# A decoder layer on one core: the chunk stage's loads three chunks ahead, its exponential sums from a store, and the modulation vectors made in the pair stage

## The chip, the cores and the metric

The kernel runs on one core of one Trainium2 chip. The metric is device microseconds of one execution; the median of three runs is 2089.88 us (2089.57 to 2091.57).

A core has a matrix engine (TensorE, PE in the profile; its weight loads are PEld), an elementwise engine (VectorE, DVE), an engine for functions of one input (ScalarE, ACT), a slower general one (GpSimd, POOL), and SyncE (SP), whose queue issues all of this kernel's loads and stores. Each engine runs its own queue in order, and engines wait for one another by semaphores.

## The reference

One layer, 1024 positions by 1024 channels, in float32. The parts that matter here:

```python
mod = silu(c) @ ada_w + ada_b                       # 6 vectors of 1024
sh1, sc1, gt1, sh2, sc2, gt2 = split(mod, 6)
h = rmsnorm(x, mix_pre_g) * (1.0 + sc1) + sh1
z, xbc, dt_raw, sc_b, sc_c, sc_h, gates = split(h @ w_in)
y_ssd = ssd_branch(z, xbc, dt_raw, ...) @ w_ssd_out # chunked scan, below
y_sc = short_conv_branch(sc_b, sc_c, sc_h, sc_conv_w) @ w_sc_out
mix = (sigmoid(gates)[0] * y_ssd + sigmoid(gates)[1] * y_sc) @ w_o
x = x + gt1 * rmsnorm(mix, mix_post_g)
h = rmsnorm(x, ffn_pre_g) * (1.0 + sc2) + sh2
x = x + gt2 * rmsnorm(ffn(h), ffn_post_g)
```

In the scan, 32 heads in 4 groups and 8 chunks of 128 positions; per chunk, with `a_cs` the running sum of `dt * a`:

```python
decay = exp(where(causal, a_cs[l] - a_cs[s], -inf))
y_diag = ((C @ B.T) * decay) @ x                     # within the chunk
state_new = state * exp(a_cs[-1]) + (B, exp(a_cs[-1] - a_cs), x)
y_off = (C * exp(a_cs)) @ state                      # from the chunks before
```

## The kernel before, in words

Matrix products run on operands split into a rounded high part and a remainder, three products in place of one. ScalarE casts the high part (L131), VectorE subtracts (L132). The stages, by the trace:

- **Start** (0 to 100 us): x is normalised, the vectors sc1 and sh1 are made, h is transposed.
- **Pair stage** (100 to 720): 34 times two column blocks of `w_in` are multiplied with h (class `Pair`, L179 to L277). A pair forms seven block products of twelve matmuls each from seven weights: the blocks 11, 21, 22 and the differences t1, t2, t3, t4. The split weights lie in a pool with seven buffers per kind (`ws`), so the last weight of the next pair, t4, takes the buffer that the last product of the pair before still reads. The kinds follow the string at L644: z (gate of the scan), g (merge gates), s (short convolution: two pairs sch with a multiply L629, the taps L621 on ScalarE and L624 on VectorE, then a pair scb), x (the scan's input).
- **Chunk stage** (720 to 1040): 32 chunks, n = 8 g + c. `ssd_front` transposes x and forms x·dt and the scores; `ssd_decay` forms the exponentials: a tile E, a broadcast of the running sums (L711), gives Cs = exp(E) on ScalarE (L737), and is then itself turned into the decay (L745, L746); `ssd_weigh` multiplies Cs by C and E by the masked scores on VectorE (L753, L754); `ssd_back` makes y and the state (L771, L781); `ssd_square`, `ssd_norm` (L681, L683, a power on GpSimd, L686) and `ssd_late` normalise y. Between them stand twelve projections, a half at a time by the table STEPS. x, B and C of two chunks come in one load, xb (L703), the gate in another, zt (L705), both with two buffers.
- **Passage and branches** (1040 to 1435): y is reloaded and split, and multiplied with `w_ssd` and `w_sc` (names bps). A generator `extra` is stepped between products; in it the vectors gt1, sc2, sh2 and later gt2 are made: eight loads of a 128x1024 block of `ada_w`, sixteen multiply-adds into two accumulators (L333, L335), then a matmul with ones (L359) or eight transposes (L343) and a sum.
- **Feed-forward** (1435 to 2088): 22 pairs of `w_up`, then `w_down`.

The order in the queues isn't the order of the code alone: a scheduler places each instruction on its engine by its own model of when its operands are there. A tile with several buffers makes an instruction wait for the last reader of the buffer that it takes.

Of the kernel before, what the change touches and what calls it, by code (L numbers as in the profile page):

```python
# [18 lines left out]
NG = 4  # L19
# [15 lines left out]
def hybrid_kernel(ctx: ExitStack, tc: tile.TileContext, x, pack, row_p, ada_w, w_in,  # L35
# [78 lines left out]
    acs_d = dram.tile([NCH, 32, P], F32, name="acs_d")  # L114

# [209 lines left out]
    def ada_steps(i, name, rows=False):  # L325
        r = None if rows else const.tile([P, 8], F32, name=name + "_c")
        acc = [qt(f"{name}_acc{h}") for h in range(2)]
        for k in range(KT):
            pc = load_raw(ada_w[k * P:(k + 1) * P, i * D:(i + 1) * D], f"{name}_p{k}")
            for h in range(2):  # L330
                src = pc[:, h * 512:h * 512 + 512]
                if k == 0:
                    V.tensor_scalar(acc[h], src, csil[:, 0:1], None, op0=ALU.mult)  # L333
                else:
                    V.scalar_tensor_tensor(acc[h], src, csil[:, k:k + 1], acc[h], op0=ALU.mult, op1=ALU.add)  # L335
            if k % 2:
# [17 lines left out]
    def ada_gate(i, n, name, dst=None, dram_dst=None):  # L354
        for acc in ada_steps(i, name, True):
            yield
        ps = double(f"{name}_ps")
        for h in range(2):
            PE.matmul(ps[:, h, :], ones, acc[h], start=True, stop=True)  # L359
        for h in range(2):  # L360
# [4 lines left out]
            V.tensor_tensor(b, ps[:, h, :], b, op=ALU.add)  # L365
            d = dst[:, sl] if dst is not None else b
            V.tensor_tensor(d, b, g, op=ALU.mult)
            if dst is None:
                SY.dma_start(dram_dst[:, sl], b)
# [156 lines left out]
    def dt_steps():  # L526
        nega = const.tile([P, 1], F32, name="nega")
        sts = []
        for th in range(2):
# [26 lines left out]
            st = l  # L556
            V.tensor_copy(st[0:32, :], cs[0:32, :])
# [138 lines left out]
    pairs = {}  # L696

    def ssd_front(g, c):
        nm = f"{g}_{c}"
        if c % 2 == 0:  # L700
            tsl = slice(c * P, c * P + 256)
            xb = ld.tile([P, 6, 256], F32, tag="xb", name=f"xb{nm}")
            SY.dma_start(xb, xbc_d[g][:, :, tsl])  # L703
            zt = ld.tile([P, 4, 256], F32, tag="zt", name=f"zt{nm}")
            SY.dma_start(zt, z_d[g][:, :, tsl])  # L705
            pairs["in"] = xb, zt
        xb, zt = pairs["in"]
# [56 lines left out]
    def ssd_back(front, decay):  # L764
        nm, g, c, xb, zt, cs, hs, E, xdt, sm, Bt = front
        Cs, cd, xw = decay
        state = pairs.get("state")
        pt = bank(f"y{nm}")
        for j in range(4):
            def ymm(o, lhs, rhs, first, last):  # L770
                return PE.matmul(pt[o * 64:o * 64 + 64, j * P:j * P + P], lhs[:, 2 * j + o, :], rhs[:, 2 * j + o, :],  # L771
                                 start=first, stop=last)
            for o in range(2):
                ins = ymm(o, xdt, E, True, c == 0)
            if c > 0:
                for o in range(2):
                    ins = ymm(o, state, Cs, False, True)
# [577 lines left out]
```

## Time and profile before

| | us |
|---|---|
| median of three runs (range) | 2089.88 (2089.57 to 2091.57) |
| profiled execution | 2089.95 |
| its span | 2088.2 |
| TensorE busy | 2006.3 (96%) |
| VectorE busy | 1499.0 (72%) |
| ScalarE busy | 998.2 (48%) |
| GpSimd busy | 158.0 (8%) |

The span runs from the first to the last instruction; the rest of an execution's time lies around it. The shares are means over stages with different limits, and each stage has to be read alone. In a timeline row stand the start in us, the duration, the engine, the line, the operation, out<-in by the program's names without buffer numbers, and in brackets how long the engine had been idle and what released it. The granted clock of TensorE, PEclk, is 1.00 at its full speed.

### The profile page before, as it was taken

Reading aid. Unit: us, or ns where it says so; the run is one execution under the profiler, and the core shown is the slowest. Engines: PE = TensorE matmul, PEld = TensorE weight load, DVE = VectorE, ACT = ScalarE, POOL = GpSimd, SP = SyncE. Lnnn points to the kernel's source line nnn. Section 1 sums busy time; section 2 is a strip of 40 time slices with the busy share of each in tenths; the row PEclk is TensorE's granted clock in tenths of the full one; section 3 lists DMA queues with packets and bytes.
Section 4 is the critical chain, followed back from the end, with each engine's and each line's share of the span. In section 5 each row is a group of like instructions: output and inputs, shape, how many; then the busy total and the mean of one; then the engine's idle time right before and its main releaser. Section 6 shows DMA issues by size and latency. Waiting matters only on the chain. (4 is left out here: it accounts for less than half of the span.)

```text
span 2088.2 us, 25325 instructions
## 1 busy us (share of the span) xinstructions
PE 2006.3 (96%) x9404; PEld 1598.0 (77%) x9404; DVE 1499.0 (72%) x2088; ACT 998.2 (48%) x1622; POOL 158.0 (8%) x183
## 2 busy tenths in 40 slices
PE   7999999999999998899989999998999999989997
PEld 3788888888888776666668878876888888868886
DVE  4977565677677688888787465368978777867876
ACT  4655344455445475656442253236545445544343
POOL 2200000000000033332100010013000000000002
PEclk9999999999999999989999999999999999999999
DMA  8223323232332455545588478343222222268372
GB/s 299 78 103 123 119 93 131 101 111 96 116 121 102 151 192 185 171 159 187 178 290 289 148 244 300 112 148 116 91 81 81 81 91 81 71 229 289 107 236 96
DMA packets 129580, 313.18 MB, mean 150 GB/s; under 512 B 11312, under 2 KB 40368, under 8 KB 129456
## 3 DMA queue, kind: packets, MB, share of 16 engines
q1 hardware_dynamic: 129456, 311.56, 42.9%
q8 instruction: 74, 1.21, 0.2%
q14 instruction: 50, 0.41, 0.1%
HBM read 243.75 MB, written 67.76 MB: 149 GB/s over the span
## 5 line engine op out<-in xcount | busy, mean ns | idle before, releaser
L1080 DVE SCALAR_TENSOR_TENSOR uv<-u_u,pk,uv 128x1023 f32<-128x1023 f32 (+1 forms) x88 | 107.2, 1278 | 7.4 <-ACT uv L1077 7.4
L131 ACT CAST u_t_hi<-u_t 128x512 fp32r<-128x512 f32 x88 | 54.7, 623 | 120.5 <-PE u_p L173 108.6
L131 ACT CAST wy_hi<-wy_raw 128x1024 fp32r<-128x1024 f32 x32 | 33.6, 1051 | 131.2 <-PE bps L896 94.3
L595 DVE SCALAR_TENSOR_TENSOR xv<-x_u,pk,xv 128x1023 f32<-128x1023 f32 (+2 forms) x72 | 87.1, 1278 | 4.9 <-ACT xv L592 4.9
L745 ACT ACTIVATE E<-E,tokS 128x128 f32<-128x128 f32 x256 | 79.4, 390 | 16.0 <-DMA E<-acs_d 15.6
L131 ACT CAST u_hi<-u_raw 128x512 fp32r<-128x512 f32 x66 | 41.0, 623 | 72.7 <-PE u_p L173 72.7
L132 DVE TENSOR_TENSOR u_t_lo<-u_t,u_t_hi 128x512 fp32r<-128x512 f32 x88 | 60.2, 687 | 21.3 <-ACT u_t_hi L131 21.1
L771 PE MATMUL y<-E,xdt 128*64 128x128 f32 x512 | 66.6, 294 | 5.1 <-issue 5.0
L132 DVE TENSOR_TENSOR wy_lo<-wy_raw,wy_hi 128x1024 fp32r<-128x1024 f32 x32 | 39.0, 1220 | 40.0 <-ACT wy_hi L131 40.0
L771 PE MATMUL y<-Cs,state 128*64 128x128 f32 x448 | 61.5, 291 | 0.0
L737 ACT ACTIVATE Cs<-E 128x1024 f32<-128x1024 f32 x28 | 29.6, 1056 | 61.2 <-DMA E<-acs_d 61.2
L131 ACT CAST x_t_hi<-x_t 128x512 fp32r<-128x512 f32 x48 | 30.0, 624 | 59.2 <-PE x_p L173 33.8
L771 PEld LDWEIGHTS y<-E,xdt 128*64 128x64 f32 x512 | 44.4, 143 | 17.7 <-issue 14.9
L1077 ACT ACTIVATE uv<-u_u,pk 128x1024 f32<-128x1024 f32 x44 | 52.5, 1239 | 2.3 <-DVE u_u L261 1.7
L1227 POOL TENSOR_TENSOR dss<-dss,dss 128x1 f32<-128x1 f32 x8 | 3.8, 476 | 623.6 <-PE dx L1155 600.2
L668 POOL MEMSET mask<- 128x128 f32 x1 | 0.2, 204 | 656.4 <-PE x_p L174 656.4
L131 ACT CAST x_hi<-x_raw 128x512 fp32r<-128x512 f32 x36 | 22.5, 624 | 52.8 <-PE x_p L173 25.0
L132 DVE TENSOR_TENSOR x_t_lo<-x_t,x_t_hi 128x512 fp32r<-128x512 f32 x48 | 32.4, 686 | 21.1 <-ACT x_t_hi L131 21.1
L771 PEld LDWEIGHTS y<-Cs,state 128*64 128x64 f32 x448 | 45.2, 145 | 2.3 <-issue 1.7
L132 DVE TENSOR_TENSOR u_lo<-u_raw,u_hi 128x512 fp32r<-128x512 f32 x66 | 44.9, 682 | 2.5 <-ACT u_hi L131 2.5
L257 DVE TENSOR_TENSOR u_u<-u_p,u_q 128x512 f32<-128x512 f32 x22 | 15.2, 691 | 43.9 <-PE u_p L174 43.9
L743 POOL TENSOR_TENSOR xw<-xdt,tokS 128x512 f32<-128x512 f32 x28 | 41.8, 1496 | 46.7 <-DVE xdt L718 46.7
(1985 smaller groups left out, 6808.6 us busy)
## 6 DMA issues: line engine op xcount, KB each, us to landing
u_raw<-in_w_up_dram SPq DMA_DIRECT2D x44, 512.0 KB, 3.5
E<-acs_d SPq DMA_DIRECT2D x32, 512.0 KB, 4.5
wy_raw<-in_w_ssd_dram SPq DMA_DIRECT2D x32, 512.0 KB, 5.0
x_raw<-in_w_in_dram SPq DMA_DIRECT2D x24, 512.0 KB, 3.5
xbc_d<-xv SPq DMA_DIRECT2D x24, 512.0 KB, 2.8
xb<-xbc_d SPq DMA_DIRECT2D x16, 768.0 KB, 5.4
f_d<-uv SPq DMA_DIRECT2D x22, 512.0 KB, 2.6
dm<-f_d SPq DMA_DIRECT2D x44, 256.0 KB, 6.0
```

Of the source, the lines that this page charges most:

```text
L131: S.copy(hi, src)
L132: V.tensor_sub(lo, src, hi.bitcast(F32))
L257: V.tensor_tensor(self.out(1, 1), self.bank(1), self.q["5"], op=ALU.add)
L595: V.scalar_tensor_tensor(v[:, s:], u[:, :T - s], w[:, k:k + 1], v[:, s:], op0=ALU.mult, op1=ALU.add)
L668: G.memset(mask, 1.0)
L737: S.activation(Cs, E, AF.Exp)
L743: G.tensor_tensor(xw, xdt, bc(tS[:, 3, hs], 64), op=ALU.mult)
L745: S.activation(E[:, h, :], E[:, h, :], AF.Relu, scale=-1.0, bias=tS[:, 0, g * 8 + h:g * 8 + h + 1])
L771: return PE.matmul(pt[o * 64:o * 64 + 64, j * P:j * P + P], lhs[:, 2 * j + o, :], rhs[:, 2 * j + o, :], start=first, stop=last)
L1077: S.activation(v, us[j], AF.Identity, scale=w[:, 2:3], bias=cv["ffn_b"][:, t:t + 1])
L1080: V.scalar_tensor_tensor(v[:, s:], us[j][:, :T - s], w[:, k:k + 1], v[:, s:], op0=ALU.mult, op1=ALU.add)
L1227: G.tensor_tensor(ss, ss, other, op=ALU.add)
```

## The change

It has three parts. In the chunk stage E is loaded three chunks ahead, in two halves of 256 KB that live in a pool with ten buffers; xb is loaded a pair of chunks earlier and has three buffers; zt one pair earlier. E's exponential and its product with the mask are done by halves. Cs is no longer computed from E: a second store in DRAM, eac_d, holds exp of the running sums, written in `dt_steps` by one ScalarE operation per half of the sequence, and Cs (two buffers as before) is a broadcast load of it, issued behind `ssd_back` for the chunk two ahead. The vectors gt1, sc2, sh2 and gt2 are made in the pair stage by the generator `mods`, stepped twice after every pair but the x pairs, the scb pairs and the first two; a half vector is eight multiply-adds into the one tile `scratch`, from four loads of 128x2x512, and a matmul with ones or four transposes. gt1 goes to DRAM (g1_d) and is reloaded before the output product. And the first three weights of the branches are loaded at the end of the chunk stage.

```diff
+    def ada_half(i, h, name):
+        for p in range(KT // 2):
+            pc = evt(f"{name}_p{p}").rearrange("p (m c) -> p m c", m=2)
+            SY.dma_start(pc, ada_w[p * 256:(p + 1) * 256, i * D + h * 512:i * D + h * 512 + 512]
+                         .rearrange("(m p) c -> p m c", p=P))
+            for m in range(2):
+                k = 2 * p + m
                 if k == 0:
+                    V.tensor_scalar(scratch, pc[:, m, :], csil[:, 0:1], None, op0=ALU.mult)
                 else:
+                    V.scalar_tensor_tensor(scratch, pc[:, m, :], csil[:, k:k + 1], scratch, op0=ALU.mult, op1=ALU.add)
+            if p < KT // 2 - 1:
+                yield
+    def ada_mod(i, r, name):
         for h in range(2):
+            yield from ada_half(i, h, f"{name}{h}")
+            ps = bank(f"{name}_ps{h}")
+            for j in range(4):
+                PE.transpose(ps[:, j * P:(j + 1) * P], scratch[:, j * P:(j + 1) * P], ident)
...
-    def ada_gate(i, n, name, dst=None, dram_dst=None):
+    def ada_gate(i, n, name, dst):
         for h in range(2):
+            yield from ada_half(i, h, f"{name}{h}")
+            ps = bank(f"{name}_ps{h}")
+            PE.matmul(ps, ones, scratch, start=True, stop=True)
...
+            kept(S.activation(e[0:32, :], cs[0:32, :], AF.Exp))
+            SY.dma_start(eac_d[th * 4:th * 4 + 4].rearrange("c h l -> h c l"),
+                         e[0:32, :].rearrange("h (c l) -> h c l", c=4))
...
+    def mods():
+        yield from ada_gate(2, 0, "gt1", g1_d)
+        yield from ada_mod(4, mod2["sc2"], "sc2")
+        plus_one(mod2["sc2"], "ffn_pre_g")
+        yield from ada_mod(3, mod2["sh2"], "sh2")
+        yield from ada_gate(5, 1, "gt2", g_d)
+    mod_it = mods()
+    for n, kind in enumerate("zzgsgsgsgsgsgsggxxzxzxxzxxzxxzxxzx"):
         fn, g, j = dict(z=zs, x=xs, g=gs, s=scs)[kind].pop(0)
         fn(g, j)
+        if n > 1 and kind != "x" and not (kind == "s" and g):
+            next(mod_it, None)
+            next(mod_it, None)
...
+            xb = ld.tile([P, 6, 256], F32, tag="xb", name=f"xb{g}_{c}", bufs=3)
...
+                t = qt(f"E{g}_{c}_{q}")
+                SY.dma_start(t, acs_d[c, h0:h0 + 4, :].rearrange("h l -> (h l)").partition_broadcast(P))
...
+            Cs = sw.tile([P, 8, P], F32, tag="Cs", name=f"Cs{g}_{c}", bufs=2)
+            SY.dma_start(Cs.rearrange("p h l -> p (h l)"),
+                         eac_d[c, g * 8:g * 8 + 8, :].rearrange("h l -> (h l)").partition_broadcast(P))
...
-            S.activation(Cs, E, AF.Exp)
...
-        S.activation(E, E, AF.Exp, scale=-1.0)
-        return Cs, cd, xw
+        for q in range(2):
...
+            S.activation(E[q], E[q], AF.Exp, scale=-1.0)
...
-        V.tensor_tensor(E, E, sm.unsqueeze(1).to_broadcast([P, 8, P]), op=ALU.mult)
+        for q in range(2):
+            V.tensor_tensor(E[q], E[q], sm.unsqueeze(1).to_broadcast([P, 4, P]), op=ALU.mult)
...
     for n in range(len(chunks)):
         this = front, decay
+        load_sums(n + 3)
+        if n % 2 == 0:
+            load_x_pair(n + 2)
+        else:
+            load_z_pair(n + 1)
...
         ssd_back(*this)
+        if n:
+            load_decay(n + 2)
...
+    pre = {(1, 0, h): load_raw(w_ssd[h * 8], f"wy1_0_{h}") for h in range(2)}
+    pre[1, 0, 2] = load_raw(w_sc[0], "ws1_0")
...
-        yield from ada_gate(2, 0, "gt1", dst=G1)
-        for nm, i in (("sc2", 4), ("sh2", 3)):
...
-        yield from ada_gate(5, 1, "gt2", dram_dst=g_d)
```

What this does to the order in the queues, at three places. The numbers behind the names count the program's tiles; lines are those of the kernel that the rows are from (each stands two lower in the changed one up to the pairs).

First, VectorE's queue around the seam from pair sch1 to pair g4 (t3_lo and t4_lo belong to g4, scb0 is the pair behind it), before:

```order
L132 TENSOR_TENSOR g4_t3_lo_1668<-g4_t3_1665,g4_t3_hi_1667 128x512
L194 TENSOR_TENSOR scb0_t2_1810<-scb0_1_raw_1794,scb0_t1_1804 128x512
L132 TENSOR_TENSOR g4_t4_lo_1674<-g4_t4_1671,g4_t4_hi_1673 128x512
L629 TENSOR_TENSOR sch1_u0_1569<-sch1_u0_1569,sch1_u1_1570 128x1024
L194 TENSOR_TENSOR scb0_t3_1820<-scb0_1_raw_1794 128x512
L624 SCALAR_TENSOR_TENSOR sch1_u1_1570<-sch1_u0_1569,pk_75,sch1_u1_1570 128x1023
L624 SCALAR_TENSOR_TENSOR sch1_u1_1570<-sch1_u0_1569,pk_75,sch1_u1_1570 128x1022
```

And in the changed kernel, where the L337 operations are the sums of the half gt1_ps1:

```order
L134 TENSOR_TENSOR g4_t3_lo_1726<-g4_t3_1723,g4_t3_hi_1725 128x512
L196 TENSOR_TENSOR scb0_t2_1876<-scb0_1_raw_1860,scb0_t1_1870 128x512
L337 SCALAR_TENSOR_TENSOR scratch_172<-gt11_p2_1669,csil_170,scratch_172 128x512
L134 TENSOR_TENSOR g4_t4_lo_1732<-g4_t4_1729,g4_t4_hi_1731 128x512
L631 TENSOR_TENSOR sch1_u0_1608<-sch1_u0_1608,sch1_u1_1609 128x1024
L337 SCALAR_TENSOR_TENSOR scratch_172<-gt11_p2_1669,csil_170,scratch_172 128x512
L196 TENSOR_TENSOR scb0_t3_1886<-scb0_1_raw_1860 128x512
L626 SCALAR_TENSOR_TENSOR sch1_u1_1609<-sch1_u0_1608,pk_75,sch1_u1_1609 128x1023
L337 SCALAR_TENSOR_TENSOR scratch_172<-gt11_p3_1673,csil_170,scratch_172 128x512
L626 SCALAR_TENSOR_TENSOR sch1_u1_1609<-sch1_u0_1608,pk_75,sch1_u1_1609 128x1022
L337 SCALAR_TENSOR_TENSOR scratch_172<-gt11_p3_1673,csil_170,scratch_172 128x512
L366 TENSOR_TENSOR gt1_b1_1679<-gt1_ps1_1677,gt1_b1_1679 128x512
```

Four sums of the half came in, three of them behind g4's t4_lo, and the last two behind a tap each. TensorE's queue at the same seam, before (the first three are the last of sch1, the others the first of g4):

```order
L172 MATMUL sch1_p1_1526<-h22_7h_542,sch1_t4_hi_1522 128x512
L173 MATMUL sch1_p1_1526<-h22_7l_543,sch1_t4_hi_1522 128x512
L174 MATMUL sch1_p1_1526<-h22_7h_542,sch1_t4_lo_1523 128x512
L172 MATMUL g4_p1_1677<-h11_0h_561,g4_11_hi_1641 128x512
L173 MATMUL g4_p1_1677<-h11_0l_562,g4_11_hi_1641 128x512
```

And changed:

```order
L174 MATMUL sch1_p1_1565<-h22_7h_544,sch1_t4_hi_1561 128x512
L175 MATMUL sch1_p1_1565<-h22_7l_545,sch1_t4_hi_1561 128x512
L176 MATMUL sch1_p1_1565<-h22_7h_544,sch1_t4_lo_1562 128x512
L361 MATMUL gt1_ps1_1677<-scratch_172,ones_82 128x512
L174 MATMUL g4_p1_1735<-h11_0h_563,g4_11_hi_1699 128x512
L175 MATMUL g4_p1_1735<-h11_0l_564,g4_11_hi_1699 128x512
```

The matmul that reads scratch stands between the pairs; the same holds for gt1_ps0 (before g2), sc2_ps0 (before sch2), sc2_ps1 (sch3), sh2_ps0 (scb2), sh2_ps1 (x0_0), gt2_ps0 (x1_0) and gt2_ps1 (x2_2).

Second, VectorE's queue at a seam behind a g pair, from g6 to sch2 (g8 follows), before:

```order
L132 TENSOR_TENSOR sch2_t3_lo_2113<-sch2_t3_2110,sch2_t3_hi_2112 128x512
L194 TENSOR_TENSOR g8_t2_2244<-g8_1_raw_2228,g8_t1_2238 128x512
L132 TENSOR_TENSOR sch2_t4_lo_2119<-sch2_t4_2116,sch2_t4_hi_2118 128x512
L194 TENSOR_TENSOR g8_t3_2254<-g8_1_raw_2228 128x512
L132 TENSOR_TENSOR g8_11_lo_2231<-g8_0_raw_2226,g8_11_hi_2230 128x512
```

And changed, with the last four sums of sc2_ps0 and their reduction (L347):

```order
L134 TENSOR_TENSOR sch2_t3_lo_2193<-sch2_t3_2190,sch2_t3_hi_2192 128x512
L196 TENSOR_TENSOR g8_t2_2332<-g8_1_raw_2316,g8_t1_2326 128x512
L337 SCALAR_TENSOR_TENSOR scratch_172<-sc20_p2_2148,csil_170,scratch_172 128x512 x2
L134 TENSOR_TENSOR sch2_t4_lo_2199<-sch2_t4_2196,sch2_t4_hi_2198 128x512
L337 SCALAR_TENSOR_TENSOR scratch_172<-sc20_p3_2152,csil_170,scratch_172 128x512
L196 TENSOR_TENSOR g8_t3_2342<-g8_1_raw_2316 128x512
L337 SCALAR_TENSOR_TENSOR scratch_172<-sc20_p3_2152,csil_170,scratch_172 128x512
L347 TENSOR_REDUCE sc2_c_902<-sc2_ps0_2156 128x4
```

Two sums stand ahead of t4_lo and two behind it. Third, SP's queue in the chunk stage (group 1), before:

```order
L711 DMA E1_2_6632<-acs_d_167 128x1024
L711 DMA E1_3_6730<-acs_d_167 128x1024
L833 DMA ysc_d4_104<-scu4_6360 128x1024
L694 DMA y_d0_96<-yo0_6_6462 512x1x256
L703 DMA xb1_4_6833<-xbc_d1_89 128x6x256
L705 DMA zt1_4_6835<-z_d1_93 128x4x256
L711 DMA E1_4_6837<-acs_d_167 128x1024
```

And changed:

```order
L720 DMA xb1_4_6987<-xbc_d1_89 128x6x256
L737 DMA E1_6_0_7092<-acs_d_167 128x512
L745 DMA Cs1_3_6981<-eac_d_168 128x1024
L737 DMA E1_6_1_7094<-acs_d_167 128x512
L875 DMA ysc_d4_104<-scu4_6594 128x1024
L711 DMA y_d0_96<-yo0_6_6703 512x1x256
L737 DMA E1_7_0_7170<-acs_d_167 128x512
L745 DMA Cs1_4_7090<-eac_d_168 128x1024
```

The load of E is two to three chunks further on, in halves, and the load of Cs, which is new, runs between them for a nearer chunk.

## Rows read from the trace of the kernel before

**Rows 1.** Three stretches: length, each engine's busy us (instructions), PEclk, DMA share, GB/s

```profile
100.00:720.00 620.00, 620.00 (x2720) 507.31 (x2721) 410.91 (x561) 298.19 (x449) 0.00 (x0) 1.00 0.31 112
720.00:1040.00 320.00, 291.11 (x1942) 217.71 (x1941) 267.43 (x503) 191.65 (x431) 90.11 (x86) 0.96 0.54 181
1075.00:1435.00 360.00, 356.14 (x1584) 289.88 (x1582) 213.08 (x265) 122.50 (x162) 26.91 (x36) 1.00 0.61 210
```

**Rows 2.** Timeline of TensorE and ScalarE, seam from pair sch to g

```profile
299.82 0.39 PE L172 MATMUL g_p<-h_0h,g_hi 128*128 128x512 f32 x1
...
299.79 0.62 ACT L131 CAST g_t_hi<-g_t 128x512 fp32r<-128x512 f32 x1 [2.10 <-PE sch_p L173]
```

**Rows 3.** Timeline of VectorE at the same seam

```profile
300.45 0.69 DVE L132 TENSOR_TENSOR g_t_lo<-g_t,g_t_hi 128x512 fp32r<-128x512 f32 x1 [1.13 <-ACT g_t_hi L131]
301.06 1.22 DVE L629 TENSOR_TENSOR sch_u<-sch_u,sch_u 128x1024 f32<-128x1024 f32 x1
...
303.50 1.28 DVE L624 SCALAR_TENSOR_TENSOR sch_u<-sch_u,pk,sch_u 128x1023 f32<-128x1023 f32 x1 [0.62 <-ACT sch_u L621]
```

**Rows 4.** Timeline of TensorE and VectorE, seam from a g pair to scb

```profile
318.99 0.39 PE L172 MATMUL scb_p<-h_0h,scb_hi 128*128 128x512 f32 x1
...
319.61 0.69 DVE L132 TENSOR_TENSOR scb_t_lo<-scb_t,scb_t_hi 128x512 fp32r<-128x512 f32 x1 [1.13 <-ACT scb_t_hi L131]
320.34 0.69 DVE L194 TENSOR_TENSOR g_t<-g_raw 128x512 f32<-128x512 f32 x1
```

**Rows 5.** Vector work: timeline of two sums; lines L359, L343 (ns min/median/max)

```profile
1063.02 1.40 DVE L335 SCALAR_TENSOR_TENSOR gt_acc<-gt_p_raw,csil,gt_acc 128x512 f32<-128x512 f32 x2
...
L359 PE MATMUL gt_ps<-gt_acc,ones x8: 590/591/592, 1079.7 to 1297.6; 128*128 128x512 f32 x8
...
L343 PE MATMUL sc_ps<-ident,sc_acc x8: 270/272/275, 1119.2 to 1120.0; 128*128 128x128 f32 x8
```

**Rows 6.** Stretches in and behind TensorE's idle times, columns as in rows 1

```profile
792.70:797.80 5.10, 0.01 (x1) 0.04 (x1) 3.67 (x7) 3.11 (x9) 0.00 (x0) 0.65 0.88 266
794.20:804.40 10.20, 6.61 (x41) 5.26 (x41) 6.12 (x14) 4.28 (x11) 1.97 (x2) 0.50 0.35 116
921.20:922.60 1.40, 0.09 (x1) 0.12 (x2) 1.40 (x4) 1.40 (x5) 0.04 (x1) 1.00 0.91 265
923.90:927.30 3.40, 3.40 (x27) 2.73 (x22) 3.38 (x6) 2.85 (x7) 0.30 (x1) 0.51 0.75 247
1041.90:1049.00 7.10, 4.51 (x18) 3.46 (x19) 7.08 (x10) 6.84 (x11) 0.00 (x0) 1.00 0.71 222
1060.50:1070.70 10.20, 4.98 (x11) 3.53 (x12) 9.12 (x14) 1.04 (x1) 0.00 (x0) 0.50 0.90 296
```

**Rows 7.** Waits from 735 to 1040: engine, line, releaser, us, times, longest

```profile
DVE ym L683 <- PE half L681: 27.2, 21, 3.7
DVE rs L686 <- POOL yr L122: 12.8, 29, 1.2
DVE Cs L753 <- ACT Cs L737: 5.5, 2, 5.1
...
PE xT L716 <- DMA xb<-xbc_d: 14.8, 12, 5.1
...
SPq L711 <- PE y L771: 84.6, 20, 9.6
```

**Rows 8.** Timeline in the chunk stage: mask product, y, Cs two chunks on

```profile
1018.13 1.22 DVE L754 TENSOR_TENSOR E<-E,sm 128x1024 f32<-128x1024 f32 x1
...
846.08 0.48 PE L771 MATMUL y<-Cs,state 128*64 128x128 f32 x3
...
858.49 1.21 DVE L753 TENSOR_TENSOR Cs<-Cs,xb 128x1024 f32<-128x1024 f32 x1
```

**Rows 9.** DMA issues of the page: count, KB each, median us to landing

```profile
E<-acs_d SPq DMA_DIRECT2D x32, 512.0 KB, 4.5
```

**Rows 10.** Timeline of TensorE at the start of the branches

```profile
1064.94 0.79 PE L895 MATMUL bps<-ys_0h,ws_hi 128*128 128x512 f32 x1 [6.58 <-ACT ws_hi L131]
1066.94 0.80 PE L897 MATMUL bps<-ys_0h,ws_lo 128*128 128x512 f32 x1 [0.78 <-DVE ws_lo L132]
```

More of the change, by code (lines that the diff above doesn't have):

```diff
@@ L114, in hybrid_kernel @@
     acs_d = dram.tile([NCH, 32, P], F32, name="acs_d")
+    eac_d = dram.tile([NCH, 32, P], F32, name="eac_d")
+    g1_d = dram.tile([P, D], F32, name="g1_d")
     def rstd_from(ms, name, ready=False):
@@ L364, in ada_gate @@
             SY.dma_start(g, row_p[2 * n + 1, sl].partition_broadcast(P))
[L365 to L369, printed above, removed]
+            V.tensor_tensor(b, ps, b, op=ALU.add)
+            V.tensor_tensor(b, b, g, op=ALU.mult)
+            SY.dma_start(dst[:, sl], b)
             yield
@@ L643, in hybrid_kernel @@
     gs = [(gate_pair, 0, 2 * n) for n in range(8)]
-    for kind in "zzgsgsgsgsgsgsggxxzxzxxzxxzxxzxxzx":
+    mod2 = {nm: const.tile([P, 8], F32, name=f"{nm}_c") for nm in ("sc2", "sh2")}
+    def mods():
[6 more added lines that the diff above has]
+    for n, kind in enumerate("zzgsgsgsgsgsgsggxxzxzxxzxxzxxzxxzx"):
         fn, g, j = dict(z=zs, x=xs, g=gs, s=scs)[kind].pop(0)
         fn(g, j)
+        if n > 1 and kind != "x" and not (kind == "s" and g):
+            next(mod_it, None)
+            next(mod_it, None)
         if steps is not None:
@@ L650, in hybrid_kernel @@
             last[1] = steps is not None
+    for _ in mod_it:
+        pass
     ph.close()
@@ L694, in ssd_late @@
             SY.dma_start(y_d[g][:, :, (c - 1) * P:(c + 1) * P], yo)
-    pairs = {}
-    def ssd_front(g, c):
-        nm = f"{g}_{c}"
[L700 to L707, printed above, removed]
+    pairs, loaded = {}, {}
@@ new lines, in hybrid_kernel, with load_x_pair, load_z_pair @@
+    chunks = [(g, c) for g in range(NG) for c in range(NCH)]
+    def load_x_pair(n):
+        if n < len(chunks):
+            g, c = chunks[n]
+            xb = ld.tile([P, 6, 256], F32, tag="xb", name=f"xb{g}_{c}", bufs=3)
+            SY.dma_start(xb, xbc_d[g][:, :, c * P:c * P + 256])
+            loaded["x", n] = loaded["x", n + 1] = xb
+    def load_z_pair(n):
+        if n < len(chunks):
+            g, c = chunks[n]
+            zt = ld.tile([P, 4, 256], F32, tag="zt", name=f"zt{g}_{c}")
+            SY.dma_start(zt, z_d[g][:, :, c * P:c * P + 256])
+            loaded["z", n] = loaded["z", n + 1] = zt
@@ L708, in ssd_front @@
+    def ssd_front(n):
+        g, c = chunks[n]
+        nm = f"{g}_{c}"
+        xb, E, Cs = loaded.pop(("x", n)), loaded.pop(("E", n)), loaded.pop(("C", n), None)
         cs = slice((c % 2) * P, (c % 2) * P + P)
         hs = slice(g * 8, g * 8 + 8)
-        E = ld.tile([P, 8, P], F32, tag="E", name=f"E{nm}")
-        SY.dma_start(E.rearrange("p h l -> p (h l)"),
-                     acs_d[c, hs, :].rearrange("h l -> (h l)").partition_broadcast(P))
         tS = tokS[:, c]
@@ L839, in hybrid_kernel @@
     proj = projections()
-    chunks = [(g, c) for g in range(NG) for c in range(NCH)]
-    front = ssd_front(0, 0)
+    load_x_pair(0)
+    for n in range(3):
+        load_sums(n)
+        load_decay(n)
+    load_z_pair(0)
+    front = ssd_front(0)
     decay = ssd_decay(front)
@@ L909, in branch_weights @@
     def branch_weights(th, i, h):
-        if i == 0 and h == 1 and not th:
-            return load_split(None, f"wy{th}_{i}_{h}", ahead_raw[0])
-        return load_split(w_ssd[h * 8 + i], f"wy{th}_{i}_{h}")
+        src = w_sc[i] if h == 2 else w_ssd[h * 8 + i]
+        return load_split(src, f"wb{th}_{i}_{h}", pre.pop((th, i, h), None))
     def branches(th, Ay, As, extra, first=()):
@@ L1000, in mod_steps @@
         SY.dma_start(ysc_d[KT - 1], tail[0])
-        yield from ada_gate(2, 0, "gt1", dst=G1)
-        for nm, i in (("sc2", 4), ("sh2", 3)):
-            for mod2[nm] in ada_steps(i, nm):
-                yield
-            if nm == "sc2":
-                plus_one(mod2[nm], "ffn_pre_g")
+        yield
     def late_steps(xn):
```

83 lines of the change are left out of this document (37 added, 46 removed).

## The prediction

> **What bounds the kernel now.** I first cut the span into the kernel's stages and read the busy time of each engine in each [rows 1]. In the pair stage (100 to 720 us) TensorE is busy for all 620.00 us; VectorE works 410.91 and ScalarE 298.19. The reader is to see that this stage has no slack on TensorE: whatever makes it wait there makes the kernel longer. In the chunk stage (720 to 1040) TensorE has 291.11 of 320 and VectorE 267.43, so neither fills it and the waits between the engines decide. In the branches (1075 to 1435) TensorE is full again, 356.14 of 360. The change works on the chunk stage, where there is idle time, and pays for it in the pair stage, where there is none.
>
> Second, I read the seam between two pairs in the timeline of three engines [rows 2, 3]. TensorE goes from the last product of pair sch to the first of pair g without a gap: g starts at 299.82. The seven weight buffers of a pair make the cast of the next pair's t4 wait on ScalarE until TensorE's last reads (2.10 us, released by the L173 matmul), and VectorE's t4_lo, which needs that cast, starts only at 300.45, that is, after TensorE has already gone on. Today nobody on TensorE is waiting for t4_lo so soon. After an s pair the multiply L629 follows it to about 302.2, and the first tap L624 waits for ScalarE's L621 and starts at 303.50. After a g pair [rows 4] it is the same up to t4_lo at 319.61, with t3 at 320.34; TensorE goes on at 318.99.
>
> Third, TensorE's idle stretches with the clock granted beside and behind them [rows 6], and last the waits of the chunk stage and of the passage to the branches [rows 7 to 10].
>
> **Modulation vectors in the pair stage: the stall.** Each of the eight halves adds eight sums into the one tile scratch, and then TensorE reads scratch: a ones-matmul for gt1 and gt2, four transposes for sc2 and sh2. In the changed order this TensorE work stands in all eight cases exactly between the last matmul of one pair and the first of the next. The last sums of the half, though, stand on VectorE behind the next pair's t4_lo: two of them after a g pair, three after a z pair, and after an s pair two (sch0) or three (sch1) mixed with the multiply and the taps. Both queues run in order, so TensorE must stand still until the last sum. Two sums took 1.40 us [rows 5], 0.70 each; the t3 difference takes 0.6 to 0.69, a tap 1.2 net.
> - sch0 to g2: multiply to 302.2; one sum and t3 fit before the tap at 303.50; tap to 304.7; sum to 305.4. TensorE was free at 299.82: 5.6 us.
> - sch1 to g4: one more tap and one more sum: 5.6 + 1.2 + 0.7 = 7.5 us.
> - four seams after g pairs (g6, g8, g10, g14): t4_lo to about 320.3, sum 321.0, t3 321.6, sum 322.3, less 318.99: 3.3 us each, 13.2.
> - two seams after z pairs (z1_2, z2_2): one more sum, 4.0 each, 8.0.
>
> Together 5.6 + 7.5 + 13.2 + 8.0 = **+34.3**. Bounds: 26, 1 us less at each seam, since the ends of TensorE's rows are modelled and its free moment with them; 45, if each seam slips by the length of one more tap, 1.3.
>
> **The same: the clock.** The granted clock has two levels in the rows, 2.4 GHz (shown as 1.00) and 1.2 GHz (0.50). Behind 5.1 us without TensorE (792.7) it was 0.50 for 10.2 us. Behind 1.3 idle of 1.4 (921.2) it was 0.51 for 3.4 us. But 2.6 idle within 1041.9 to 1049.0 left it at 1.00 [rows 6]. In a stage where TensorE is full, 10.2 us at half clock lose 5.1. So the two long stalls (5.6 and 7.5) cost 5.1 each, 10.2; the six short ones (3.3 and 4.0) lie between rows that show nothing and rows that show a whole drop, so between 0 and 5.1, and I take half, 2.55: 15.3. Together **+25.5** (bounds 10.2 and 40.8).
>
> The rule of the Trainium skill that bears on this ("TensorE: Matmul & The Clock Gate", section "Part 1: The HAM clock gate") is that the slow clock is the default and that activity lifts it. By the rule each stall of this size could put TensorE back to the slow level, by the row at 1041.9 a short one need not; the first is a rival below.
>
> **The same: the work itself.** TensorE: 8 × 0.590 + 16 × 0.272 = 9.1 us [rows 5] leave one full stage and enter another: 0. VectorE: 64 sums × 0.70 = 44.8 us come to 410.91 of 620, and fit but for the last sums counted above; in the branches, where VectorE had 213.08 of 360, their going frees nothing that TensorE waited for. The 32 loads of 512 KB move to a stage where the DMA engines are 0.31 busy [rows 1]; the extra exponential of each half of the sums goes to ScalarE, at 298 of 620. I cost these at 0; if the loads were late, the sums would be, and the stall would grow, which the bound of 45 holds.
>
> **Chunk stage.** VectorE idles 320.00 − 267.43 = 52.6 us there. The largest parts [rows 7]: 27.2 for the squares' sum on TensorE (ym, 21 times), 12.8 for the power on GpSimd (rs, 29 times), 5.5 for ScalarE's exponential Cs. TensorE's own largest wait is 14.8 us for the pair load xb, 12 times, up to 5.1 us, and ym stands behind it in TensorE's queue. With xb loaded a pair earlier the 14.8 go, and I let ym fall by as much (bounds 0, if something else is late next, and 27.2). The 28 exponentials leave ScalarE, so the 5.5 go. The power (rs) is not touched. The mask product of E is cut in two, 64 of half the width: full width lasts 1.22 [rows 8] and half width 0.69 [rows 3], each overlapping the next by 0.08 (300.45 to 301.06), so 32 × (2 × 0.61 − 1.14) = +2.6. Sum −14.8 − 5.5 + 2.6 = **−17.7** (bounds +20, see rival D, and −52.6 + 12.8 + 2.6 = −37.2).
>
> The new load of Cs could become a wait. It goes out after y of the chunk two before, and has to be there when VectorE weighs it. TensorE's y ended at 846.56 in one chunk, and the Cs of two chunks on was weighed at 858.49 [rows 8]: 11.9 us, and the loads of E, of the same size, land in 4.5 [rows 9]. Normally no wait, so 0; the longest hold of SP on y was 9.6 [rows 7], and 9.6 + 4.5 = 14.1 would be 2.2 late.
>
> **Passage to the branches.** TensorE waits 6.58 us for ws_hi and 0.78 for ws_lo [rows 10], since the raw weight is issued late; and it then runs 10.2 us at 0.50 with 4.98 busy [rows 6], 2.5 lost. With the first three weights loaded before the stage this is 9.9 at most; VectorE is full there (9.12 of 10.2) and keeps a little: **−9** (bounds 0 and −12).
>
> **The sum.** The profiled execution took 2089.95 us (span 2088.2), 0.07 over the median of three runs. 2089.95 + 34.3 + 25.5 − 17.7 − 9 = **2123 us**.
>
> **Rivals.**
> B. Every one of the eight stalls drops the clock for 10.2 us: 40.8 in place of 25.5, **2138 us**. For it: the stretch at 921.2 fell to 0.51 after 1.3 us; against it: the one at 1041.9 did not.
> C, the other side. The chunk stage loses all of VectorE's idle time but rs (−37.2) and the passage its 9, while the stalls cost their 34.3 and the clock stays: 2089.95 + 34.3 − 37.2 − 9 = **2078 us**. It decides as soon as the savings exceed the stalls with their clock. For it: the loads were what ScalarE and TensorE waited for most in this stage. Against: TensorE has 291.11 us of work in the 320 at a clock of 0.96, so that a saving of 37 would need its idle time to go altogether; and the two long stalls are longer than the 5.1 us that dropped the clock at 792.7.
> D. The load of Cs takes the place of the wait removed: with two buffers it can't be ahead. 2.2 us late in each of 28 chunks would be 62; a third of them, 20, eats the 17.7 and leaves +2.3: 2089.95 + 34.3 + 25.5 + 2.3 − 9 = **2143 us**. Against it: the 11.9 us of slack.
>
> **How the numbers follow.** Forecast 0.66, with its own range of 2105 to 2141 (the stall's 8 to 10 and the clock's 15 to either side, added as squares). B 0.12, C 0.11, D 0.07; the last 0.04 lies between C and the forecast, near no change. About 0.2%, 4.2 us, is what a measurement of this kernel can tell from none: 2085.7 to 2094.1. So faster 0.11 (C), same 0.04, slower 0.85. The range of 8 in 10 leaves out C's 2078 and what lies above D's middle: 2086 to 2152.
>
> **What would show it.** Right: TensorE waits named gt_ps, sc_ps and sh_ps for VectorE's scratch, eight of 3 to 8 us between 100 and 720, and slices with a lower granted clock there, where there is none now; no wait for xb or for ws_hi; a chunk stage of some 300 us. The forecast is wrong if these eight waits are under 1 us (TensorE's order or VectorE's then isn't what decides), if the chunk stage falls below 285 us, or if VectorE's weighing waits for the load of Cs many times.

## The result, and the profile after

The changed kernel takes 2124.01 us (median of 4 runs, 2123.52 to 2127.86), the kernel before beside it 2090.73: a ratio of 1.0163, 95% interval 1.0145 to 1.0180. The forecast was 2123 us in a range of 2086 to 2152. The profiled execution has a span of 2122.0 us, 33.8 more than before. To see where the 33.8 lie, I cut both traces at the same events of TensorE: the last matmul of the first two column blocks (zps), of the last x pair, of the chunk stage, of the output product (ops), and of `w_down` (dx), which ends the feed-forward.

| stage, us | before | after | difference |
|---|---|---|---|
| pairs | 644.7 | 702.5 | +57.8 |
| chunks | 320.1 | 310.2 | −9.9 |
| branches and output product | 378.1 | 363.4 | −14.7 |
| feed-forward | 661.7 | 661.8 | +0.1 |

These sum to 33.3; the other 0.5 lies ahead of the first event and behind the last. The stretches with these bounds, columns as in rows 1, first of the kernel before, then of after:

```profile
77.10:721.80 644.70, 644.70 (x2828) 527.21 (x2827) 432.60 (x598) 317.15 (x483) 0.00 (x0) 1.00 0.30 109
721.80:1041.90 320.10, 291.19 (x1941) 217.74 (x1940) 265.63 (x501) 190.92 (x430) 90.11 (x86) 0.96 0.54 183
1041.90:1420.00 378.10, 363.98 (x1593) 294.96 (x1594) 230.12 (x291) 132.88 (x175) 19.49 (x28) 0.99 0.63 216
```

```profile
77.40:779.90 702.50, 664.84 (x2852) 537.42 (x2850) 480.99 (x676) 318.74 (x490) 0.00 (x0) 0.97 0.37 131
779.90:1090.10 310.20, 289.98 (x1940) 215.08 (x1940) 268.33 (x533) 173.11 (x432) 83.29 (x86) 0.98 0.73 230
1090.10:1453.50 363.40, 357.08 (x1570) 291.56 (x1570) 182.49 (x212) 132.60 (x175) 19.46 (x27) 1.00 0.51 173
```

In the pair stage of after TensorE, which had no idle time there before, lacks 702.50 − 664.84 = 37.7 us, and its mean clock is 0.97. TensorE's waits of after between 100 and 720 us (engine, line, releaser, us in total, times, longest) name all of it:

```profile
PE gt_ps L361 <- DVE scratch L337: 24.1, 4, 8.5
PE sc_ps L346 <- DVE scratch L337: 6.8, 2, 3.5
PE sh_ps L346 <- DVE scratch L337: 6.7, 2, 3.4
```

Eight waits, 37.6 us, at the eight seams. The longest, from sch1 to g4, in the timelines of after; TensorE, ScalarE, then VectorE:

```profile
192.85 0.39 PE L176 MATMUL sch_p<-h_7h,sch_t_lo 128*128 128x512 f32 x1
201.70 1.22 PE L361 MATMUL gt_ps<-scratch,ones 128*128 128x512 f32 x1 [8.47 <-DVE scratch L337]
```

```profile
193.09 0.62 ACT L133 CAST g_t_hi<-g_t 128x512 fp32r<-128x512 f32 x1 [2.35 <-PE sch_p L175]
...
196.66 1.15 ACT L623 ACTIVATE sch_u<-sch_u,pk 128x1024 f32<-128x1024 f32 x1 [2.47 <-DVE sch_u L631]
```

```profile
194.14 0.75 DVE L337 SCALAR_TENSOR_TENSOR scratch<-gt_p,csil,scratch 128x512 f32<-128x512 f32 x1 [1.46 <-DMA gt_p<-in_ada_w_dram]
194.81 0.68 DVE L134 TENSOR_TENSOR g_t_lo<-g_t,g_t_hi 128x512 fp32r<-128x512 f32 x1
195.41 1.22 DVE L631 TENSOR_TENSOR sch_u<-sch_u,sch_u 128x1024 f32<-128x1024 f32 x1
196.55 0.75 DVE L337 SCALAR_TENSOR_TENSOR scratch<-gt_p,csil,scratch 128x512 f32<-128x512 f32 x1
...
197.85 1.28 DVE L626 SCALAR_TENSOR_TENSOR sch_u<-sch_u,pk,sch_u 128x1023 f32<-128x1023 f32 x1
199.05 0.74 DVE L337 SCALAR_TENSOR_TENSOR scratch<-gt_p,csil,scratch 128x512 f32<-128x512 f32 x1
199.71 1.27 DVE L626 SCALAR_TENSOR_TENSOR sch_u<-sch_u,pk,sch_u 128x1022 f32<-128x1022 f32 x1
200.91 0.74 DVE L337 SCALAR_TENSOR_TENSOR scratch<-gt_p,csil,scratch 128x512 f32<-128x512 f32 x1
```

This is read from the bottom up: the last sum ends at 201.65 and TensorE starts at 201.70; ahead of that sum stands a tap, ahead of it a sum, and so on back to t4_lo. No row has a gap ahead of it but the first: that sum waited 1.46 us for its load, landed after the cast was done (193.71), and t4_lo behind it started 1.1 us later than it could have.

Behind the waits, the clock. Stretches of after, columns as in rows 1; the first four follow or end the waits at 146, 193, 264 and 308, the next two those at 352 and 413, the last two those at 514 and 637:

```profile
148.70:155.50 6.80, 3.76 (x7) 2.35 (x8) 5.56 (x7) 1.52 (x2) 0.00 (x0) 0.50 0.19 77
196.50:206.70 10.20, 5.00 (x10) 3.28 (x11) 6.53 (x9) 2.93 (x6) 0.00 (x0) 0.50 0.22 83
268.20:271.60 3.40, 3.40 (x10) 2.63 (x9) 0.37 (x1) 0.00 (x0) 0.00 (x0) 0.50 0.02 5
312.60:316.00 3.40, 3.40 (x10) 2.66 (x9) 0.32 (x2) 0.19 (x1) 0.00 (x0) 0.50 0.00 0
355.20:359.00 3.80, 3.80 (x19) 3.23 (x20) 0.69 (x1) 0.60 (x2) 0.00 (x0) 1.00 0.19 79
416.80:420.50 3.70, 3.70 (x19) 3.13 (x20) 0.86 (x2) 0.50 (x1) 0.00 (x0) 1.00 0.20 81
517.40:524.20 6.80, 6.04 (x12) 4.13 (x13) 2.09 (x3) 0.00 (x0) 0.00 (x0) 0.50 0.25 96
640.30:647.10 6.80, 4.73 (x9) 3.12 (x10) 3.36 (x5) 0.00 (x0) 0.00 (x0) 0.50 0.33 132
```

TensorE was busy for 26.3 us in the six lines at 0.50, of which half, 13.2, is lost. A part of each drop falls into the wait itself and costs nothing: in the second line TensorE works only 5.00 of 10.20.

The chunk stage of after, its largest waits (compare rows 7):

```profile
PE half L708 <- ACT Bt L770: 8.2, 9, 2.5
...
DVE ym L700 <- PE half L698: 17.0, 27, 2.4
DVE rs L703 <- POOL yr L124: 13.8, 32, 1.1
...
ACT E L785 <- DMA E<-acs_d: 35.6, 30, 3.3
ACT cd L779 <- DMA Cs<-eac_d: 17.3, 15, 4.4
```

The same wait for Bt in the kernel before:

```profile
PE half L691 <- ACT Bt L728: 3.0, 4, 1.3
```

TensorE's wait for xb is gone and VectorE doesn't wait for Cs or E; the wait for ym has shrunk from 27.2 to 17.0, and TensorE waits longer for ScalarE's Bt. In the second longest of these waits Bt stands behind an E that ScalarE had waited for (ScalarE's rows first, then TensorE's):

```profile
1000.30 1.28 ACT L785 ACTIVATE E<-E,tokS 128x128 f32<-128x128 f32 x4 [1.98 <-DMA E<-acs_d]
...
1002.67 0.25 ACT L770 COPY Bt<-half 128x128 f32<-128x128 f32 x1
```

```profile
1002.97 0.49 PE L708 MATMUL half<-rs,ones 128*128 128x128 f32 x2 [2.29 <-ACT Bt L770]
```

At the start of the branches no wait for a weight is left; the longest is 1.73 us for the first y.

### The profile page after: what moved, and what is told of

It is laid out like the page before. It is cut to its first block, busy times and chain, and to the rows that moved or that the text cites. A ratio compares the mean times of both kernels' runs of the same rounds, so it can differ in the third digit from the quotient of the medians.

```text
span 2122.0 us, 25489 instructions
## 1 busy us (share of the span) xinstructions
PE 2016.9 (95%) x9404; PEld 1601.2 (75%) x9404; DVE 1502.5 (71%) x2120; ACT 981.8 (46%) x1630; POOL 150.6 (7%) x183
## 5 line engine op out<-in xcount | busy, mean ns | idle before, releaser
L134 DVE TENSOR_TENSOR wb_lo<-wb_raw,wb_hi 128x1024 fp32r<-128x1024 f32 x44 | 53.8, 1223 | 87.6 <-ACT wb_hi L133 83.7
L133 ACT CAST wb_hi<-wb_raw 128x1024 fp32r<-128x1024 f32 x44 | 46.3, 1052 | 137.8 <-PE bps L951 129.6
L785 ACT ACTIVATE E<-E,tokS 128x128 f32<-128x128 f32 x256 | 83.8, 391 | 47.8 <-DMA E<-acs_d 35.6
L133 ACT CAST x_t_hi<-x_t 128x512 fp32r<-128x512 f32 x48 | 29.9, 624 | 59.2 <-PE x_p L175 33.8
L988 DVE SCALAR_TENSOR_TENSOR gt<-gt,bps 128x512 f32<-128x512 f32 x32 | 20.6, 684 | 50.8 <-PE bps L952 47.5
L800 ACT ACTIVATE scratch<-yo 128x512 f32<-128x512 f32 x32 | 20.1, 628 | 58.7 <-DVE yo L843 58.7
L259 DVE TENSOR_TENSOR u_u<-u_p,u_q 128x512 f32<-128x512 f32 x22 | 15.2, 691 | 43.9 <-PE u_p L176 43.9
L795 DVE TENSOR_TENSOR E<-E,sm 128x512 f32<-128x512 f32 x64 | 43.7, 699 | 0.0
```

The costliest lines, as they stand in the source:

```text
L133: S.copy(hi, src)
L134: V.tensor_sub(lo, src, hi.bitcast(F32))
L259: V.tensor_tensor(self.out(1, 1), self.bank(1), self.q["5"], op=ALU.add)
L785: S.activation(E[q][:, h, :], E[q][:, h, :], AF.Relu, scale=-1.0, bias=tS[:, 0, g * 8 + q * 4 + h:g * 8 + q * 4 + h + 1])
L795: V.tensor_tensor(E[q], E[q], sm.unsqueeze(1).to_broadcast([P, 4, P]), op=ALU.mult)
L800: S.activation(sq, y2, AF.Square, scale=512 ** -0.5)
```

## The experiments

The question was first whether the terms of the sum are where the forecast put them, and then which part of the change makes the chunk stage shorter. The table has all stages by the same events, in us, with the ratio to the kernel before and its interval. The runs were made in three groups, e, f and g, each with the kernel before beside it, which had medians of 2088.8 to 2093.3; so times of different groups are compared by their ratios. A stage's length comes from one traced execution. The chunk stages of after and e4 have the same code but for the early loads at the end, and differ by 2.8 us; smaller differences of that stage between two runs show nothing.

| run | pairs | chunks | branches | median | ratio (95%) |
|---|---|---|---|---|---|
| after | 702.5 | 310.2 | 363.4 | 2124.01 | 1.0163 (1.0145 to 1.0180) |
| e1_mods_only | 701.1 | 321.8 | 365.8 | 2138.05 | 1.0213 (1.0193 to 1.0232) |
| e2_chunk_only | 645.5 | 309.9 | 379.2 | 2081.75 | 0.9945 (0.9923 to 0.9967) |
| e3_delayed | 651.4 | 310.3 | 363.0 | 2074.30 | 0.9909 (0.9892 to 0.9926) |
| e4_no_early_weights | 703.8 | 313.0 | 362.9 | 2128.66 | 1.0171 (1.0151 to 1.0190) |
| f1_xb_late | 650.7 | 324.5 | 361.9 | 2084.06 | 0.9976 (0.9966 to 0.9987) |
| f2_cs_by_scalar | 650.7 | 310.2 | 362.9 | 2071.73 | 0.9912 (0.9897 to 0.9927) |
| f3_sums_two_ahead | 650.7 | 310.3 | 361.8 | 2071.72 | 0.9916 (0.9901 to 0.9930) |
| f4_no_early_weights | 650.7 | 311.2 | 362.6 | 2074.40 | 0.9927 (0.9912 to 0.9942) |
| g1_xb_early_alone | 644.8 | 315.7 | 377.8 | 2085.56 | 0.9973 (0.9960 to 0.9986) |
| g2_xb_and_delayed | 650.7 | 315.9 | 366.4 | 2077.80 | 0.9934 (0.9914 to 0.9955) |
| g3_delayed_cs_two_ahead | 650.7 | 308.1 | 365.8 | 2069.79 | 0.9896 (0.9875 to 0.9918) |

**The modulation part alone (e1).** The kernel before with the functions ada_half, ada_mod, ada_gate and mods of the change and the shorter generators in the branches; nothing else of it.

> The kernel before with one part of the change alone: the modulation vectors made in the pair stage; the chunk stage and the branches' first weights as before. Theory (TensorE stands at eight seams until the last sums in scratch, and the clock falls after it): the pair stage is 58 us longer, as in the changed kernel, the branches lose the 9 us of TensorE work that moved: 2090.7 + 58 - 9 = 2140 us, eight waits of TensorE for scratch of 3 to 8.5 us. Rival (the loss comes from the new loads of the chunk stage, or from the extra DMA and exponentials of the sums, and the waits at the seams are hidden): 2082 to 2095.

The pair stage is 56.4 us longer and TensorE's waits there are those of after (24.3, 6.8 and 6.7 us). The time is 2138.05. The whole loss of the change comes with this part. The branches are shorter in it too, 365.8 for 378.1, without any early weight.

**The chunk part alone (e2).** The changed kernel with the functions of before for the modulation:

```diff
-        if n > 1 and kind != "x" and not (kind == "s" and g):
-            next(mod_it, None)
-            next(mod_it, None)
...
+        yield from ada_gate(2, 0, "gt1", dst=G1)
+        for nm, i in (("sc2", 4), ("sh2", 3)):
+            for mod2[nm] in ada_steps(i, nm):
+                yield
```

> The changed kernel with the modulation vectors back in the branches, made as before: the chunk stage's loads, the store of exponentials and the early weights alone. Theory: the chunk stage keeps its 10 us and the passage some 5 to 6: 2090.7 - 10 - 5.6 = 2075 us, no idle time of TensorE in the pair stage. Rival: 2110 or more if the chunk part carries the loss; 2063 if the forecast's own 17.7 + 9 were right and something of the modulation part hid them.

The pair stage is back at 645.5 and the chunk stage stays at 309.9: that part holds. The time, 2081.75, is 7 above what I expected, since the branches got nothing: 379.2, although their first weights were loaded early. TensorE still waits for a weight, as its waits in the branches show:

```profile
PE bps L937 <- ACT wb_hi L132: 4.3, 1, 4.3
```

**The same work, TensorE's read one pair later (e3).** The read of scratch moves into the first step of the next half, ahead of the sum that overwrites it:

```diff
     def ada_half(i, h, name, acc, before):
...
+            if p == 0 and before:
+                before.pop()()       # gt: ones-matmul; sc, sh: transposes
             for m in range(2):
...
-            if p < KT // 2 - 1:
-                yield
+            yield
```

> The changed kernel with one thing moved: TensorE reads scratch not behind the pair at which the last sums were made but behind the next pair that carries sums, just ahead of the next half's first sum. The work, the loads and the tile are the same. Theory: the eight waits (37.6 us in the trace of the changed kernel) and the clock lost behind them (half of 26 us of work at half speed, 13) go: 2124 - 37.6 - 13 = 2073 us. Rival (VectorE's 45 us of added sums or the added loads themselves slow the pair stage): the time stays above 2110, with the waits named after weights or raw tiles instead.

2074.30 us; the pair stage in this trace:

```profile
77.70:729.10 651.40, 651.30 (x2853) 530.24 (x2851) 477.19 (x676) 318.92 (x490) 0.00 (x0) 1.00 0.39 142
```

The work is that of after (2853 matmuls in the stage for 2852, 676 operations on VectorE in both, 44.6 us more than before) and so are the loads, and TensorE is busy 651.30 of 651.40 at 1.00. So neither VectorE's added work nor the loads slow the pairs. 651.4 − 644.7 = 6.7 us is the TensorE work that moved in (6.0 by the six later runs with this read, all at 650.7); the other 51.1 of the 57.8 was the seam: 37.6 of waiting, and 13.5 left for the clock, where the rows above give 13.2.

**Without the early weights (e4, and f4 on the kernel of e3).**

```diff
-    pre = {(1, 0, h): load_raw(w_ssd[h * 8], f"wy1_0_{h}") for h in range(2)}
-    pre[1, 0, 2] = load_raw(w_sc[0], "ws1_0")
+    pre = {}
```

> The changed kernel without the early loads of the branches' first three weights. Theory (the early weights gave the passage its 5.6 us): 2124 + 6 = 2130 us, with TensorE's wait for a weight of some 6 us back at the start of the branches. Rival (what shortened the passage is that the modulation vectors' loads and sums no longer stand ahead of the weights there): 2124, no such wait.

> The kernel with the delayed read (2074.3 us) without the early loads of the branches' first three weights. Theory, after the run without them in the changed kernel showed no wait for a weight: the passage is short because the modulation's loads and sums are gone from it, and this is 2073 to 2077. Rival (the forecast's: the early weights give some 6 to 9): 2080 to 2083.

The branches take 362.9 and 362.6 us without the early weights, 363.4 and 363.0 with them, and no wait for a weight appears; the longest of e4 there is the one for the first y:

```profile
PE bps L949 <- ACT y_0h L943: 1.7, 1, 1.7
```

e4's median is 4.6 higher, but its trace has that in the pairs and the chunks, and its ratio (1.0171) lies within the interval of after; f4 is at 2074.40. The rival of e4 and the theory of f4, which say the same, hold: what shortened the passage is that the loads and sums of the modulation no longer stand in it. e1 and e2 show it from the other side: modulation moved without early weights, 365.8; early weights with the modulation in its old place, 379.2, no gain.

**xb late again (f1).** On the kernel of e3, the pair's load where it was, with two buffers:

```diff
-        if n % 2 == 0:
-            load_x_pair(n + 2)
-        else:
-            load_z_pair(n + 1)
+        if n % 2:
+            load_x_pair(n + 1)
+            load_z_pair(n + 1)
```

> The kernel with the delayed read of scratch (2074.3 us, chunk stage 310.3) with one thing undone: x, B and C of two chunks are loaded when their pair begins, in two buffers as before. Theory (the earlier load of xb is what shortened the chunk stage): TensorE waits for xb again, 10 to 15 us in some 12 places, the stage is 318 to 322 us and the time 2082 to 2086. Rival (the exponentials taken off ScalarE did it): 2074 to 2077.

The chunk stage is 324.5, and the waits of TensorE and VectorE in it are

```profile
PE xT L761 <- DMA xb<-xbc_d: 11.8, 12, 3.1
...
DVE ym L703 <- PE half L701: 34.2, 30, 3.8
```

That is 14.2 us longer than in e3, and 4.4 longer than before. TensorE's wait for xb and the time are as the theory said; the stage is 2.5 us longer than its range. The load of zt isn't a part of this: "The change" says that it goes out a pair earlier, but it is issued in the same step of the loop as before (`load_z_pair(n + 1)` at odd n).

**Cs by ScalarE (f2), E two chunks ahead (f3), both (g3).** On the kernel of e3:

```diff
+            for q in range(2):
+                S.activation(Cs[:, q * 4:q * 4 + 4, :], E[q], AF.Exp)      # f2, g3: no eac_d
...
-        load_sums(n + 3)
+        load_sums(n + 2)                                                   # f3, g3
```

> The kernel with the delayed read (2074.3 us) with one thing undone: Cs is again exp(E) on ScalarE, in two halves, the store of exponentials and its 28 loads are left out. Forecast's theory (the exponentials on ScalarE held up VectorE for 5.5 us): 2078 to 2080. Rival (the loads of Cs hold SP until y is done and so make E late, 46 us of ScalarE's waits for E, behind which Bt and then TensorE stand, 6.7 us): without them 2068 to 2071.

> The kernel with the delayed read (2074.3 us) with E loaded two chunks ahead in place of three. Theory (ScalarE takes each E as soon as it lands and has time, so the distance moves only where ScalarE waits): within 2 us of 2074. Rival (the third chunk of lead covers the holds of SP): 2078 to 2085, and VectorE waiting for E.

> The kernel with the delayed read, Cs by ScalarE again and E two chunks ahead: both undone together. Theory (neither is worth anything, singly or together): chunk stage 308 to 312, ratio to the kernel before 0.990 to 0.992. Rival (the one covers for the other): chunk stage above 314, ratio above 0.994.

Chunk stages of 310.2, 310.3 and 308.1 against 310.3: neither the store of exponentials nor the third chunk of lead is worth anything, and neither costs anything that these runs can tell. In f2 TensorE's wait for Bt falls from 6.7 to 3.5 us and the stage stays as long, so that wait isn't what holds the stage at 310. The forecast's theory for f2 falls; its rival, that the Cs loads cost 3 to 6, isn't shown either (2071.73, but at the same ratio as e3). g3, with both undone, has the lowest time of the study, 2069.79 us, but its ratio, 0.9896 (0.9875 to 0.9918), can't be told from that of e3.

**xb early on the kernel before (g1), and with the delayed modulation (g2).**

```diff
+            xbs.append(ld.tile([P, 6, 256], F32, tag="xb", name=f"xb{g}_{c}", bufs=3))
+            SY.dma_start(xbs[-1], xbc_d[g][:, :, c * P:c * P + 256])
...
+        if n % 2 == 0:
+            load_x_pair(n + 2)
```

> The kernel before with one thing changed: the load of x, B and C of two chunks goes out a pair earlier, with three buffers (the state's tiles move to another pool to make room). E, Cs, the modulation and the weights are as before. Theory (this load alone is the chunk stage's gain, 14 us by the run that undid it): chunk stage 304 to 307 in place of 320.1, ratio to the kernel before 0.993 to 0.994. Rival (the gain needs E's lead or the store as well): 314 to 320, ratio above 0.997.

> The kernel before with the earlier xb as in the run beside it and the modulation vectors in the pair stage with TensorE's read delayed; E, Cs and the first weights as before. Theory (nothing else in the change is worth anything, and E's halves and the new loads cost some 4): chunk stage 304 to 307, branches 363, so some 4 us under the kernel with the delayed read: ratio to the kernel before 0.987 to 0.990. Rival (E's lead and the store belong to the gain): above 0.992.

My theory after f1 falls in both: 315.7 and 315.9, not 304 to 307, and by the numbers both rivals hold (of the store that they name, f2 shows that it isn't needed). With xb early the wait for ym is down to 11.7, and the wait for E is the largest that e3 doesn't have:

```profile
DVE ym L683 <- PE half L681: 11.7, 25, 1.4
DVE E L759 <- ACT E L751: 7.3, 3, 6.5
```

6.51 of the 7.3 us are one wait, for the first chunk. The kernel before has it under another name, as 5.06 of the 5.5 us for Cs [rows 7]: there ScalarE made the Cs of the second chunk, the first that has one, ahead of the first E's exponential, and in both VectorE waits for ScalarE's first results of the stage. The first row is g1, the second the kernel before:

```profile
739.07 1.23 DVE L759 TENSOR_TENSOR E<-E,sm 128x1024 f32<-128x1024 f32 x1 [6.51 <-ACT E L751]
737.47 1.23 DVE L753 TENSOR_TENSOR Cs<-Cs,xb 128x1024 f32<-128x1024 f32 x1 [5.06 <-ACT Cs L737]
```

ScalarE starts on the first E at 731.50 in the kernel before, 9.7 us behind the pairs' end, and at 727.37 in e3, 1.7 us ahead of it:

```profile
731.50 0.40 ACT L745 ACTIVATE E<-E,tokS 128x128 f32<-128x128 f32 x1 [0.52 <-DMA E<-acs_d]
727.37 1.57 ACT L788 ACTIVATE E<-E,tokS 128x128 f32<-128x128 f32 x5
```

So the two loads act at two places, which the start of the first y tells apart:

| run | E | xb | pairs' end to first y | first y to the stage's end |
|---|---|---|---|---|
| before | as before | late | 18.4 | 301.6 |
| g1_xb_early_alone | as before | early | 19.0 | 296.7 |
| g2_xb_and_delayed | as before | early | 18.3 | 297.6 |
| f1_xb_late | early | late | 13.6 | 310.9 |
| e3_delayed | early | early | 13.7 | 296.5 |
| after | early | early | 15.1 | 295.1 |

In all runs with E early the first part is 13.5 to 15.2 us, in the others 18.3 to 22.0 (e1). In all runs with xb early the second part is 294.4 to 297.8, in the others 299.8 (e1) to 310.9. E's early load gives some 5 us at the start, the early xb some 5 behind it, and that makes the 10. Of E's load the lead, the halves and the pool of their own were not tried apart.

## Why the prediction was right

The sum came out at +33.1 and the profile has +33.8, but two of its terms missed by 8 and 12 us in opposite directions. The way and the rough size follow from the stall, whose mechanism was right; that the sum is right to 1 us is luck. Of the signs named, the eight waits (the longest 8.5 us, not 8), the lower clock and the missing waits for xb and ws_hi came; the chunk stage of some 300 us didn't.

- **The stall**: forecast 34.3, measured 37.6. Seam by seam: sch0 5.6 against 5.74, sch1 7.5 against 8.47, after g pairs 3.3 each against 3.46, 3.37, 3.37 and 3.37, after z pairs 4.0 each against 4.69 and 5.17. The mechanism was right to the instruction, and e3 shows it: the same work read a pair later costs 6.7 us in all. At sch1 a late load comes on top: the sum ahead of t4_lo waited 1.46 us for it, and t4_lo with it.
- **The clock**: forecast 25.5, measured 13.2 to 13.5. This is the step that was most wrong in size. I put a whole 10.2 us at half speed behind each long wait and half of that behind each short one. The long ones had drops of 6.8 and 10.2, begun while TensorE was still waiting, so that the two lost 1.9 and 2.5 us (half of 3.76 and 5.00). Of the short ones the four after g pairs had 3.4 us twice and none twice; the two after z pairs had 6.8 each, begun in the wait, and lost 3.0 and 2.4. The rival that every wait costs a full drop is refuted: by the row at 355.20 a 3.37 us wait left the clock at 1.00, and only one drop lasted 10.2 us. The rule of the Trainium skill ("TensorE: Matmul & The Clock Gate", section "Part 1: The HAM clock gate") is that the slow clock is the default and activity lifts it. The trace agrees as far as the clock fell at six of the eight waits and rose again behind each of the six.
- **The moved work**: costed at 9.1 both ways from the durations; 6.0 to 6.7 in the traces, since successive matmuls overlap (in e3 two records of 0.59 us for gt_ps start 0.43 us apart, at 165.47 and 165.90). That it cancels wasn't measured by itself.
- **The chunk stage**: forecast −17.7, measured −9.9. The step that failed is that ym falls by the 14.8 us of xb: it fell by 10.2, and xb early on the kernel before shortens the part behind the first y by 4.9 (g1). The 5.5 us for Cs did go, but not for the reason given: with the exponentials back on ScalarE (f2) they don't come back. They were two waits, and 5.06 of them one at the start of the stage, when ScalarE had begun on the first E 9.7 us behind the pairs' end; E now comes earlier, and at least 26 of the 28 exponentials had no part in it. The product by halves was about right: E's mask product takes 43.7 us in after and 41.4 before, 2.3 for the 2.6. The fear of rival D, that the load of Cs becomes a wait, didn't come true for VectorE or TensorE; ScalarE's small copy of it waits, 17.3 us, and without these loads (f2) the stage is as long.
- **The passage**: forecast −9; of the −14.7 of the branches 6.7 are the moved work, which leaves −8.0. The size was right and the cause wrong: e1, e2, e4 and f4 show that the early weights give nothing that can be told, and that the gain comes with moving the modulation out.
- **The other side** (rival C) would have needed the chunk stage to give 37. It gave 9.9, and no run of the study gave more than 12.0 (g3).

What stays open: why the part behind the first y is 9.3 us longer in f1 than in the kernel before, though xb comes late in both, so that the early xb is worth 14 us there and 5 on the kernel before. VectorE's wait for ym has 7.0 of it (34.2 for 27.2); no run shows what stands behind.

## What to carry to other kernels

Where one engine is full, look at where in its queue a new instruction stands, not at how much work it brings: matmuls that take 6.7 us cost 57.8 because they read a sum whose last terms stood behind the next pair's weights on another engine, and one pair of delay took that back. A sum over stages can come out right with wrong terms; only runs with single parts undone showed that the early weights and the store of exponentials were worth nothing. And look at where in a stage a wait lies before you divide it among the chunks: the 5.5 us for Cs looked like a price of 28 exponentials and were in the main one wait at the start, behind a late load.

## What the runs showed of the hardware that was not expected

Waits of TensorE of equal length didn't cost the same. In the traces of after, e1 and e4 twelve waits of 3.4 us between busy stretches were followed by 3.4 us at half clock six times, and by none six times; all twelve waits of 4.4 us or more were followed or overlapped by 3.4 to 10.2 us at half clock. Even there the loss in work was mostly smaller than half of the drop's length, since in eleven of the twelve the drop had begun during the wait.
